# A hybrid encoder layer on one core: recurrence pairs issued in five parts between half lumps of a weight fold, decays in five slices

## The chip, the core and the metric

The kernel runs on one core of a Trainium2 chip. Times are device microseconds from start to end of one execution. The kernel before took 2605.68 us (median of 3 runs, 2604.11 to 2606.04). The core has a matrix engine (PE, whose weight loads PEld overlap its matmuls), a vector engine (DVE), an activation engine (ACT), GpSimd (POOL), and SyncE (SP), whose queue issues nearly all of this kernel's DMAs. Each engine works through its own instructions in order and waits on semaphores for the others.

## What is computed

One encoder layer on 2048 frames of width 1024, in float32: token mixing (sliding-window attention with sinks beside a gated linear recurrence, HGRN2), cross-attention into 256 memory tokens, and a SwiGLU feed-forward part, each with an RMS norm before and after. The change touches the recurrence and the weights of the cross-attention. In short:

```python
def hgrn2(q, f_logit, i, g, lb, onorm_g):          # per head, chunks of 64 frames
    f = lb + (1 - lb) * sigmoid(f_logit); k = 1 - f
    b = cumsum(log(f))                             # within a chunk
    b_mid, b_last = b[31], b[63]
    A = tril((q * exp(b - b_mid)) @ (k * exp(b_mid - b)).T)
    kv = (k * exp(b_last - b)).T @ i
    S = exp(b_last) * S_prev + kv                  # from chunk to chunk
    o = A @ i + (q * exp(b)) @ S_prev
    return rms_norm(o, onorm_g) * silu(g)

def cross_attention(u, m, wq, wk, wv, wo):         # 4 heads of width 256
    p = softmax((u @ wq) @ (m @ wk).T / 16)
    return (p @ (m @ wv)) @ wo
```

## The kernel before

All float32 matmuls of weights are made from three products of a rounded-down and a rest part (`mm3`, L156 to L163: hi x hi, hi x lo, lo x hi), so each weight tile that is loaded (`raw`) is first split: the rounded part `whi` on ACT or POOL (L143, L145), the rest `wlo` on DVE (L146).

The stages follow each other: the input projection of the first half of the frames (`in_first`); the second half's projection (`in_proj`, `in_cols`) beside the first half's attention (`swa`) and recurrence (`hgrn`); the second half's attention; then, in the stage that the change mostly concerns, the second half's recurrence beside the *fold* (`fold_cross`); and then, as a stream of large blocks (`phases`), the output projection, the cross-attention and the feed-forward part.

**The fold** multiplies the memory tokens into the cross-attention's weights ahead of time, since they are fixed: with `kT = wk.T m.T` the scores are `u @ (wq kT)`, and likewise for values. It is a generator that yields after each *lump*: 8 lumps for `kT` (tiles `mT`, 24 matmuls of 256 columns each, L161 to L163, into a bank of kind s or h), 8 lumps for `wq kT` (24 matmuls on the tiles `kv`, two banks, stored to `qk_d`), 8 for the values, and 8 for the values with `wo` (L330 to L332, stored to `vo_d`).

**The recurrence** goes over pairs of chunks (128 frames, numbers n = 8 to 15 in the second half). One step of its generator issues the state of the last pair (`hgrn_state`: L808 on PE, L809 on POOL, L810 on DVE), the front of the next pair (`hgrn_front`), the last part of the pair before (`hgrn_last`: L838 transposes, L839, the store of `sg` to `y_d`), and the output of the last pair (`hgrn_out`: L820 and L821 on PE, four squares with sums on ACT at L825, L827 and L829 on POOL for the root, and L830 on DVE, which reads the output's bank and writes `on`). The front loads `k1`, `qq`, `kk`, `v` from `z_d`, scales on POOL (L774 `qq`, L786 `q6`, L789 `kk`), makes the scores on PE (L781) with a masked copy (L782 DVE, L783 ACT), and transposes `kk` (L792) and `v` (L797), whose copies `kt` and `vt` ACT makes (L794, L799).

Banks of PSUM come in four kinds, g, t, s and h, of two each; the second half's recurrence takes g and t in turn, the fold s and h. In a pair, the kind g serves L808, one half of L781, L792 and L838; the kind t serves the other half of L781, L797, and the output. Single tiles in SBUF serve `k1`, `kk`, `v`, `sg`, `on` and `kt`; `qq`, `q6` and `vt` have two, the raw weights and their parts three.

Before the change the loop of this stage runs one recurrence step and then two lumps of the fold:

```python
for _ in self.hgrn(range(NPB, NT), "gt"):     # L247
    for _ in range(2):
        next(fold)
```

What the Python code issues is not yet the engines' order: the tile layer (`TileContext` with its own timeline, L1648) records all instructions and decides the order on each engine when the program is built. It also places the semaphores.

**The decays** (`decays`, L626 to L649) make, for one head and one half of the frames, the logarithm, its running sum within chunks, and the exponentials `G`, `G1`, `e1` and `e2`. In the first half they are issued from the `after` generator of a projection block (L563), which the stream of blocks advances step by step.

Of the kernel before, what the change touches and what calls it, by code (L numbers as in the profile page):

```python
# [14 lines left out]
AF = mybir.ActivationFunctionType  # L15
# [33 lines left out]
class Layer:  # L49
# [103 lines left out]
        self.split(raw, hi, lo, engine)  # L153
        return (hi.rearrange("p (k c) -> p k c", k=KT), lo.rearrange("p (k c) -> p k c", k=KT))

    def mm3(self, ps, pairs):  # L156

        nc = self.nc
        n = len(pairs)
        for i, ((ah, al), (bh, bl)) in enumerate(pairs):  # L160
            nc.tensor.matmul(ps, ah, bh, start=(i == 0), stop=False)  # L161
            nc.tensor.matmul(ps, ah, bl, start=False, stop=False)  # L162
            nc.tensor.matmul(ps, al, bh, start=False, stop=(i == n - 1))  # L163
# [33 lines left out]
    def mix(self):  # L197
        tc, I = self.tc, self.I
        kw = dict(reuse_waits="tile")
        with contextlib.ExitStack() as left:  # L200
# [18 lines left out]
            with tc.tile_pool(name="sw", bufs=1, side="right", **kw) as self.sw:  # L219
                self.zero_tiles()  # L220
                swa = self.swa(range(NPB), "st")
                hgrn = self.hgrn(range(NPB), "h")
                cols = self.in_proj(1, u)
                for _ in range(2):
                    next(cols)
                for _ in swa:
                    next(hgrn)
                    next(cols)
                for _ in hgrn:
                    pass  # L230
                jobs = self.jobs()
                sums = self.w_sums()
                swa = self.swa(range(NPB, NT), "sth")
                for i, _ in enumerate(swa):
                    next(cols)
                    if i:
                        self.mark()
                        for _ in range(4):
                            next(sums, None)
                for _ in cols:  # L240
                    pass
                for _ in sums:
                    pass
            phases = self.phases(jobs, None, lambda: self.io_tile("z"))
            with tc.tile_pool(name="xp", bufs=1, side="right", **kw) as self.xp:
                fold = self.fold_cross()
                for _ in self.hgrn(range(NPB, NT), "gt"):  # L247
                    for _ in range(2):
                        next(fold)
                for _ in range(8):  # L250
                    next(phases)
                for _ in fold:
                    pass
# [20 lines left out]
    def fold_cross(self):  # L274
# [9 lines left out]
        def projected(w):  # L284
            dst = [ph.tile([P, KT, M], F32R, tag=f"kv{i}", name=f"kv{i}_{self._n}") for i in range(2)]
            for j in range(KT):
                wh, wl = self.wcols(w, j, "A")
                ps = self.bank("sh"[j % 2])[:, :M]
                self.mm3(ps, [((wh[:, k, :], wl[:, k, :]), (mT[0][:, k, :], mT[1][:, k, :])) for k in range(KT)])
                nc.scalar.activation(dst[0][:, j, :], ps, AF.Copy)  # L290
                nc.vector.tensor_tensor(dst[1][:, j, :], ps, f32(dst[0][:, j, :]), ALU.subtract)
                yield dst
# [9 lines left out]
        for d in range(KT):  # L302
            th, tl = self.wcols(self.I["wq_x"], d, "A")
            o = self.io_tile("x")
            for q in range(2):
                ps = self.bank("sh"[q])
                for r in range(2):
                    h = 2 * q + r
                    self.mm3(ps[:, r * M:(r + 1) * M],
                             [((th[:, j, :], tl[:, j, :]), (kT[0][:, j, :], kT[1][:, j, :])) for j in (2 * h, 2 * h + 1)])  # L310
                sl = slice(q * 512, (q + 1) * 512)
                nc.scalar.activation(o[:, sl], ps, AF.Copy, scale=gx[:, d:d + 1])
            self.store(self.qk_d[d * P:(d + 1) * P, :], o)
            yield
        for vT in projected(self.I["wv_x"]):
            yield
        for h in range(4):
# [204 lines left out]
    def in_block(self, ca, cb, beside, get, between):  # L522
# [40 lines left out]
        def after():  # L563
# [2 lines left out]
            c0 = ca * P  # L566
            if C_FH <= c0 < C_IH:
                e = self.pair_tile()
                self.decays(0, (c0 - C_FH) // P, z[0][:, 0, :], e[:, 0, :], e[:, 1, :])
                yield  # L570
                yield
                for j in range(2):
                    sl = slice(j * 512, (j + 1) * 512)
                    nc.vector.scalar_tensor_tensor(z[0][:, 1, sl], z[0][:, 1, sl], -0.5 * float(P) ** -0.5,
                                                   e[:, 0, sl], ALU.mult, ALU.mult)
            for i, c in enumerate((ca, cb)):
                self.store(self.z_d[c * P:(c + 1) * P, 0:TB], z[0][:, i, :])
            for _ in range(3 if C_FH <= c0 < C_IH else 4):
                yield
            for n, p in x:  # L580
                self.store_transposed(self.un_d, n, self.transposed(p[:, 0, :], p[:, 1, :]))
# [11 lines left out]
    def in_cols(self, b, u, cols, e1):  # L593
# [24 lines left out]
        for i, c in enumerate(cols):  # L618
            c0 = c * P
            if C_FH <= c0 < C_IH:  # L620
                e1 = self.io_tile("x")
                self.decays(b, (c0 - C_FH) // P, z[i], e1, self.io_tile("u"))
            self.store(self.z_d[c0:c0 + P, b * TB:(b + 1) * TB], z[i])
        return e1

    def decays(self, b, h, f, e1, e2):  # L626

        nc = self.nc
        NCB = TB // 64
        nc.scalar.activation(e1, f, AF.Ln)  # L630
        for s in range(TB // 512):
            sl = slice(s * 512, (s + 1) * 512)
            nc.vector.tensor_tensor_scan(e2[:, sl], self.reset.rearrange("p a b -> p (a b)"), e1[:, sl], 0.0,
                                         ALU.mult, ALU.add)
# [5 lines left out]
                                ALU.mult, ALU.mult)  # L640
        gs = self.small("d_g", NCB)
        nc.gpsimd.tensor_tensor(gs, mid, self.dl[:, h, b * NCB:(b + 1) * NCB], ALU.add)
        g2 = gs.rearrange("p (n c) -> p n c", c=2)
        nc.scalar.activation(self.G1[:, b * NPB:(b + 1) * NPB, h], g2[:, :, 1], AF.Exp)
        nc.gpsimd.tensor_tensor(g2[:, :, 1], g2[:, :, 0], g2[:, :, 1], ALU.add)
        nc.scalar.activation(self.G[:, b * NPB:(b + 1) * NPB, h, :], g2, AF.Exp)
        nc.scalar.activation(e1, e2, AF.Exp)
        nc.scalar.activation(e2, e2, AF.Exp, scale=-1.0)
        nc.vector.scalar_tensor_tensor(f, f, 1.0, e2, ALU.subtract, ALU.mult)  # L649

    def swa_front(self, n, kinds):
# [96 lines left out]
            nc.vector.tensor_tensor(ys[a], pr[a], ys[a], ALU.add)  # L748
        self.store(self.y_d[n, :, 0:4], ys)

    def hgrn_front(self, n, kinds):
        nc, ph = self.nc, self.hg
        t0 = n * P
        z = self.z_d
# [22 lines left out]
        for i in range(2):  # L777
# [4 lines left out]
            nc.vector.copy_predicated(at[:, hs, :], self.cmask.unsqueeze(1).broadcast_to([P, 2, P]), ps[:, :, 0:P])  # L782
            nc.scalar.activation(at[0:64, hs, 64:P], ps[0:64, :, P:192], AF.Copy)  # L783

        q6 = new("q6", 2)
        nc.gpsimd.tensor_tensor(q6.rearrange("p h (c t) -> p h c t", t=64), q1.rearrange("p h (c t) -> p h c t", t=64),  # L786
                                self.G[:, n, :, :].unsqueeze(3).broadcast_to([P, 4, 2, 64]), ALU.mult)
# [9 lines left out]
            nc.tensor.transpose(ps[:, h * P:(h + 1) * P], v[:, h, :], self.ident)  # L797
        vt = new("vt", 2)
        nc.scalar.activation(vt, ps.rearrange("p (h t) -> p h t", h=4), AF.Copy)  # L799
        return q6, at, kt, vt  # L800

    def hgrn_state(self, n, kinds, kt, vt):
        nc, ph = self.nc, self.hg
# [39 lines left out]
    def hgrn(self, pairs, kinds):  # L843

        f, o = {}, {}
        for n in itertools.chain(pairs, (None, None)):
# [2 lines left out]
                W = self.hgrn_state(m, kinds, kt, vt)  # L849
            else:  # L850
                m = None
            if n is not None:
                f[n] = self.hgrn_front(n, kinds)
            if o:
                l, v = o.popitem()
                self.hgrn_last(l, kinds, *v)
            if m is not None:
                o[m] = self.hgrn_out(m, kinds, q6, at, vt, W)
            yield
# [792 lines left out]
```

## Time and profile before

| | us |
|---|---|
| median of 3 runs | 2605.68 |
| the profiled execution | 2605.43 |
| its span, first to last instruction | 2603.6 |
| PE busy | 2526.8 |
| DVE busy | 1744.2 |
| ACT busy | 1262.3 |
| POOL busy | 473.4 |
| second half's recurrence beside the fold (PE's first L781 to its last L332) | 645.7 to 794.6 |

In the views below, times are us from the start of the span. A timeline's row has start, duration, engine, line, operation, output and inputs, and in brackets the time that the engine was idle before it and what released it. A row of the chain of waits has start, duration and the link. PE's matmuls are pipelined: a row's duration is longer than its distance to the next (256 columns: 0.28 us long, 0.12 apart). PEclk is the share of its full clock that PE was granted.

### The profile page before, as it was taken

What the parts mean: (1) busy time and instruction counts of PE and PEld (TensorE: products, weight loads), DVE (VectorE), ACT (ScalarE), POOL (GpSimd) and SP (SyncE); (2) the same over time, 40 slices, a digit from 0 to 9 for tenths busy, and PEclk for the clock granted to TensorE, in tenths of its full rate; (3) what the DMA queues carried; (4) which work ended last, traced back from release to release, by engine and by line L of the source; (5) the groups of instructions that cost most, each with busy time, mean ns of one, the idle gap of its engine ahead of it and who ended that gap; (6) DMA issues with size and microseconds to landing.
All of it is one profiled execution on the core that took longest, in us unless ns stands there. A gap on an engine that the chain in (4) does not pass through costs nothing.

```text
span 2603.6 us, 34511 instructions
## 1 busy us (share of the span) xinstructions
PE 2526.8 (97%) x12160; PEld 2112.8 (81%) x12160; DVE 1744.2 (67%) x2773; ACT 1262.3 (48%) x2641; POOL 473.4 (18%) x651
## 2 busy tenths in 40 slices
PE   7989999999998999999989999999999999999998
PEld 6878788878897777888878888888888888888786
DVE  7675578887555568786885655576666656664756
ACT  5463366655554556565573333354333335443443
POOL 4240343320321324223320000000000000000022
PEclk9999999999999999999999999999999999999999
DMA  5434655484876998756994532353556434576798
GB/s 186 142 121 166 208 157 173 131 265 158 265 253 219 281 318 265 228 193 173 306 282 145 164 128 73 105 187 114 168 181 230 148 107 168 175 225 176 229 226 210
DMA packets 286350, 497.88 MB, mean 191 GB/s; under 512 B 20576, under 2 KB 143456, under 8 KB 286176
## 3 DMA queue, kind: packets, MB, share of 16 engines
q1 hardware_dynamic: 275520, 456.87, 52.4%
q0 software_dynamic: 10656, 38.80, 8.0%
q8 instruction: 96, 1.57, 0.2%
q14 instruction: 78, 0.64, 0.1%
HBM read 328.87 MB, written 166.72 MB: 190 GB/s over the span
## 4 chain that ended last, share of the span: by engine, by line
PE 80%; DMA 8%; DVE 4%; issue 3%; POOL 2%; ACT 2%; SPq 0%; DVEq 0%; POOLq 0%; ACTq 0%
PE psm L1018 22%; PE psm L1020 22%; PE psm L1019 22%; PE psg L161 2%; PE psg L163 2%; PE psg L162 2%; DMA row<-in_x_dram 1%; PE pss L1270 1%; DMA row<-h_d 1%; ACT junk L1355 1%; DMA x<-in_w_out_dram 1%; DVE S L885 1%; DMA h_d<-row 1%; DMA pair<-in_x_dram 1%; DMA kk<-z_d 1%
## 5 line engine op out<-in xcount | busy, mean ns | idle before, releaser
L1018 PE MATMUL psm<-T,S 128*128 128x512 f32 x2664 | 1034.9, 392 | 24.6 <-ACT S L882 13.5
L1019 PE MATMUL psm<-T,S 128*128 128x512 f32 x2664 | 1041.1, 391 | 0.0
L1020 PE MATMUL psm<-T,S 128*128 128x512 f32 x2664 | 1036.1, 391 | 3.8 <-DVE S L885 3.8
L1018 PEld LDWEIGHTS psm<-T,S 128*128 128x128 f32 x2664 | 502.2, 189 | 132.7 <-ACT S L882 15.3
L1020 PEld LDWEIGHTS psm<-T,S 128*128 128x128 f32 x2664 | 501.9, 188 | 111.0 <-DVE S L885 6.9
L1019 PEld LDWEIGHTS psm<-T,S 128*128 128x128 f32 x2664 | 502.3, 189 | 103.0
L882 ACT ACTIVATE S<-sum 128x512 fp32r<-128x512 f32 (+1 forms) x338 | 208.1, 619 | 341.4 <-PE psm L1020 333.1
L885 DVE TENSOR_TENSOR S<-sraw,S 128x512 fp32r<-128x512 f32 (+1 forms) x311 | 214.2, 696 | 223.4 <-ACT S L882 213.4
L885 DVE TENSOR_TENSOR S<-sum,S 128x512 fp32r<-128x512 f32 (+1 forms) x404 | 276.8, 689 | 81.6 <-ACT S L882 63.7
L1033 ACT ACTIVATE part<-psm 128x512 f32<-128x512 f32 x297 | 175.1, 592 | 178.0 <-PE psm L1020 172.8
L882 ACT ACTIVATE S<-sraw 128x512 fp32r<-128x512 f32 (+1 forms) x272 | 166.8, 617 | 156.0 <-PE psm L1020 143.0
L1384 POOL DMA_DIRECT2D row<-y_d x28 | 25.0, 892 | 1132.5 <-DMA sraw<-hid_d 964.5
L1355 ACT ACTIVATE junk<-row 128x512 f32<-128x512 f32 x160 | 99.7, 625 | 118.2 <-DVE row L1377 34.9
L885 DVE TENSOR_TENSOR T<-row,T 128x1024 fp32r<-128x1024 f32 x104 | 123.1, 1191 | 30.5 <-ACT T L882 30.2
L161 PE MATMUL psg<-u,whi 128*128 128x512 f32 x352 | 141.1, 401 | 1.6 <-POOL whi L145 1.6
L163 PE MATMUL psg<-u,wlo 128*128 128x512 f32 x352 | 139.5, 396 | 0.9 <-DVE wlo L146 0.9
L162 PE MATMUL psg<-u,whi 128*128 128x512 f32 x352 | 139.6, 396 | 0.0
L882 ACT ACTIVATE T<-row 128x1024 fp32r<-128x1024 f32 x104 | 105.7, 1027 | 20.7 <-DMA row<-in_w_down_dram 10.3
L884 POOL TENSOR_SCALAR S<-sum 128x512 fp32r<-128x512 f32 x66 | 50.5, 765 | 238.7 <-PE psm L1020 148.3
L1536 DVE TENSOR_TENSOR part<-psm,part 128x512 f32<-128x512 f32 x66 | 45.4, 688 | 65.3 <-PE psm L1020 65.2
L146 DVE TENSOR_TENSOR wlo<-raw,whi 128x1024 fp32r<-128x1024 f32 x54 | 68.7, 1271 | 29.1 <-ACT whi L143 22.4
L1527 DVE TENSOR_TENSOR row<-psm,part 128x512 f32<-128x512 f32 x66 | 45.4, 689 | 57.6 <-PE psm L1020 57.5
(329 smaller groups left out, 3651.3 us busy)
## 6 DMA issues: line engine op xcount, KB each, us to landing
sraw<-in_w_gate_dram SPq DMA_DIRECT2D x44, 512.0 KB, 4.9
sraw<-in_w_up_dram SPq DMA_DIRECT2D x44, 512.0 KB, 4.8
hid_d<-row SPq DMA_DIRECT2D x44, 512.0 KB, 2.7
h_d<-row SPq DMA_DIRECT2D x32, 512.0 KB, 6.9
y_d<-row SPq DMA_DIRECT2D x32, 512.0 KB, 3.8
sraw<-hid_d SPq DMA_DIRECT2D x32, 512.0 KB, 5.2
row<-h_d POOLq DMA_DIRECT2D x30, 512.0 KB, 7.5
row<-y_d POOLq DMA_DIRECT2D x28, 512.0 KB, 7.3
```

Of the source, the lines that this page charges most:

```text
L146: nc.vector.tensor_tensor(lo, raw, f32(hi), ALU.subtract)
L161: nc.tensor.matmul(ps, ah, bh, start=(i == 0), stop=False)
L162: nc.tensor.matmul(ps, ah, bl, start=False, stop=False)
L163: nc.tensor.matmul(ps, al, bh, start=False, stop=(i == n - 1))
L882: self.nc.scalar.activation(hi, raw, AF.Copy)
L884: self.nc.gpsimd.tensor_scalar(hi, raw, 1.0, 1.0, ALU.mult, ALU.mult)
L885: self.nc.vector.tensor_tensor(lo, raw, f32(hi), ALU.subtract)
L1018: nc.tensor.matmul(ps, s[:, 0, k, :], t[:, 0, k, :], start=st, stop=False, **kw)
L1019: nc.tensor.matmul(ps, s[:, 0, k, :], t[:, 1, k, :], start=False, stop=False, **kw)
L1020: nc.tensor.matmul(ps, s[:, 1, k, :], t[:, 0, k, :], start=False, stop=sp, **kw)
L1033: nc.scalar.activation(t, ps, AF.Copy)
L1355: self.nc.scalar.activation(junk, a, AF.Square, scale=float(D) ** -0.5, accum_out=to)
```

## The change

Four things are edited.

1. `hgrn` yields five times for a pair: after the state, in the middle of the front (which is now a generator itself and leaves its results in `f`), after the front, after the last part, and after the output. The first half's loop takes five of them where it took one.
2. The fold yields half lumps: `mm3` gets a `part` and issues half of its matmuls, `projected` yields between the halves, and the lumps of `wq kT` yield after each bank.
3. The loop of the second half advances the fold by one half lump after each of the four later parts of a pair, and by none after the state. So a pair still has four half lumps.
4. `decays` is a generator of five slices (four yields). In the first half the block's `after` advances it step by step; it had two bare yields behind the whole, and three before its next part, and now has one there. Within `decays`, the exponential `e1` comes ahead of `G`, and `G` after `e2`. `in_cols` runs it at once.

```diff
-    def mm3(self, ps, pairs):
+    def mm3(self, ps, pairs, part=None):
...
         for i, ((ah, al), (bh, bl)) in enumerate(pairs):
+            if part is not None and i * 2 // n != part:
+                continue
             nc.tensor.matmul(ps, ah, bh, start=(i == 0), stop=False)
...
                 for _ in swa:
-                    next(hgrn)
+                    for _ in range(5):
+                        next(hgrn)
                     next(cols)
...
-                for _ in self.hgrn(range(NPB, NT), "gt"):
-                    for _ in range(2):
+                for i, _ in enumerate(self.hgrn(range(NPB, NT), "gt")):
+                    for _ in range(1 if i % 5 else 0):
                         next(fold)
...
-                self.mm3(ps, [((wh[:, k, :], wl[:, k, :]), (mT[0][:, k, :], mT[1][:, k, :])) for k in range(KT)])
+                for part in range(2):
+                    if part:
+                        yield dst
+                    self.mm3(ps, [((wh[:, k, :], wl[:, k, :]), (mT[0][:, k, :], mT[1][:, k, :])) for k in range(KT)],
+                             part)
...
-            self.store(self.qk_d[d * P:(d + 1) * P, :], o)
-            yield
+                if q:
+                    self.store(self.qk_d[d * P:(d + 1) * P, :], o)
+                yield
...
-                self.decays(0, (c0 - C_FH) // P, z[0][:, 0, :], e[:, 0, :], e[:, 1, :])
-                yield
-                yield
+                yield from self.decays(0, (c0 - C_FH) // P, z[0][:, 0, :], e[:, 0, :], e[:, 1, :])
...
-            for _ in range(3 if C_FH <= c0 < C_IH else 4):
+            for _ in range(1 if C_FH <= c0 < C_IH else 4):
                 yield
...
         nc.scalar.activation(e1, f, AF.Ln)
+        yield
...
         nc.gpsimd.tensor_tensor(gs, mid, self.dl[:, h, b * NCB:(b + 1) * NCB], ALU.add)
+        yield
         g2 = gs.rearrange("p (n c) -> p n c", c=2)
         nc.scalar.activation(self.G1[:, b * NPB:(b + 1) * NPB, h], g2[:, :, 1], AF.Exp)
         nc.gpsimd.tensor_tensor(g2[:, :, 1], g2[:, :, 0], g2[:, :, 1], ALU.add)
+        nc.scalar.activation(e1, e2, AF.Exp)
+        yield
+        nc.scalar.activation(e2, e2, AF.Exp, scale=-1.0)
         nc.scalar.activation(self.G[:, b * NPB:(b + 1) * NPB, h, :], g2, AF.Exp)
-        nc.scalar.activation(e1, e2, AF.Exp)
-        nc.scalar.activation(e2, e2, AF.Exp, scale=-1.0)
+        yield
         nc.vector.scalar_tensor_tensor(f, f, 1.0, e2, ALU.subtract, ALU.mult)
...
-    def hgrn_front(self, n, kinds):
+    def hgrn_front(self, n, kinds, f):
...
             nc.scalar.activation(at[0:64, hs, 64:P], ps[0:64, :, P:192], AF.Copy)
 
+        yield
         q6 = new("q6", 2)
...
-        return q6, at, kt, vt
+        f[n] = q6, at, kt, vt
+        yield
...
                 W = self.hgrn_state(m, kinds, kt, vt)
             else:
                 m = None
-            if n is not None:
-                f[n] = self.hgrn_front(n, kinds)
+            yield
+            yield from self.hgrn_front(n, kinds, f) if n is not None else (None, None)
             if o:
                 l, v = o.popitem()
                 self.hgrn_last(l, kinds, *v)
+            yield
             if m is not None:
                 o[m] = self.hgrn_out(m, kinds, q6, at, vt, W)
             yield
```

More of the change, by code (lines that the diff above doesn't have):

```diff
@@ L621, in in_cols @@
                 e1 = self.io_tile("x")
-                self.decays(b, (c0 - C_FH) // P, z[i], e1, self.io_tile("u"))
+                for _ in self.decays(b, (c0 - C_FH) // P, z[i], e1, self.io_tile("u")):
+                    pass
             self.store(self.z_d[c0:c0 + P, b * TB:(b + 1) * TB], z[i])
```

## The prediction

> **What bounds the kernel now.** I read the page first, then PE's stretches and idle time between 640 and 810 us, then the chain of waits there, then the DMA queue's timeline. The page's chain says who sets the end:
>
> ```profile
> PE 80%; DMA 8%; DVE 4%; issue 3%; POOL 2%; ACT 2%; SPq 0%; DVEq 0%; POOLq 0%; ACTq 0%
> ```
>
> PE sets it, so an edit is worth what it takes from, or adds to, PE's holes. The tile layer chooses each engine's order when the program is built. Set side by side, the built orders of the two kernels are equal, instruction by instruction, in their tiles and in what they wait for, until the second half of the recurrence is under way beside the fold (PE's time 677 us); and they are equal again from the last part of the fold on. Only what lies between can gain or lose. PE's stretches there (us of the stretch, then busy us and instructions of each engine):
>
> ```profile
> core 0: us, PE busy (x) PEld busy (x) DVE busy (x) ACT busy (x) POOL busy (x), PEclk, DMA share, GB/s
> 687.00:692.00 5.00, 4.22 (x33) 3.75 (x33) 4.22 (x7) 0.92 (x3) 2.13 (x2) 1.00 0.46 129
> 701.00:704.00 3.00, 2.65 (x22) 2.30 (x22) 2.74 (x5) 0.69 (x1) 1.60 (x2) 1.00 1.00 325
> 713.00:715.40 2.40, 0.45 (x5) 0.25 (x4) 0.82 (x2) 0.00 (x0) 1.38 (x3) 1.00 0.36 147
> 715.40:719.30 3.90, 3.80 (x19) 3.60 (x20) 2.29 (x4) 1.91 (x6) 1.96 (x2) 0.56 0.89 268
> 720.00:757.00 37.00, 37.00 (x316) 37.00 (x315) 17.35 (x24) 21.99 (x61) 11.93 (x14) 1.00 0.79 259
> 757.00:794.50 37.50, 37.50 (x227) 33.19 (x226) 17.37 (x20) 20.20 (x31) 0.00 (x0) 1.00 0.69 239
> ```
>
> From 720 on PE has no hole. Before that there are three, and a stretch at a granted clock of 0.56 right behind the third. PE stands before the same instruction, the transposition of v (L797):
>
> ```profile
> 702.05 0.63 PE L797 MATMUL pst<-ident,v 128*128 128x128 f32 x4 [0.35 <-issue]
> ...
> 713.10 0.28 PE L163 MATMUL psh<-kv,wlo 128*128 128x256 f32 x1
> 715.33 0.55 PE L797 MATMUL pst<-ident,v 128*128 128x128 f32 x3 [1.95 <-DVE on L830]
> ```
>
> L797 needs a bank of the kind t; there are two, and the one whose turn it is still holds the outputs of the pair before, until DVE's L830 has read them. The chain of waits says why L830 is late, and, by its L808 rows, how long a pair takes:
>
> ```profile
> 697.74 0.89 PE psg L808 x8
> ...
> 704.64 6.79 DMA kk<-z_d
> 711.57 0.61 POOL kk L789
> 712.18 1.00 POOL q L786
> 713.26 0.20 POOL h_vv L827
> 713.54 1.02 POOL h_rs L829
> 714.58 0.70 DVE on L830
> 715.33 0.55 PE pst L797 x3
> ...
> 724.36 0.89 PE psg L808 x8
> ...
> 735.32 0.89 PE psg L808 x8
> ```
>
> L830 waits for L829, and L829 stands on POOL behind L789, which waits for the load of kk. L789 to L830 take 714.58 + 0.70 - 711.43 = 3.85 us from the landing.
>
> **The change part by part.** *The decays in slices, and the five parts in the first half of the recurrence.* No instruction of either stands elsewhere in the built order. Cost 0 from both sides; there is nothing that needs cover.
>
> *The five parts with half lumps, second half.* It adds no instruction and no DMA. For a pair, PE's order was: state (L808), scores (L781), 15 or 16 fold matmuls, v (L797), kk (L792), some 17 fold matmuls, L838, output (L820, L821), 16 fold matmuls. It becomes: L808, L781, 16 fold matmuls, kk, 11 fold matmuls, v, 5, L838, 4, output, 12. So L797 comes 11 fold matmuls and four transpositions later: 11 x 0.117 + 0.44 = 1.7 us (37 us for 316 matmuls; eight of L808's kind take 0.89). In the first pair L838 comes 24 fold matmuls, 2.8 us, later, and with it DVE's L839, SP's store of y_d and what stands on SP behind that store's landing (the loads of sg, k and q). PE wants those a pair later, so the slack is most of 11 us, and I cost it at 0; without that slack it would be up to 2.8. On DVE, L830 moves behind the state's sum (L810) and one split of fold weights (L146); what is now queued behind its wait is one or two short copies, no longer L810 and L146. On POOL, kk goes ahead of q in two pairs. On SP nothing is added; kk's load goes ahead of v's in most pairs, and in the first pair one load of fold weights goes ahead of kk's.
>
> What the holes cost: the pairs from 697.74 to 724.36 took 26.62 us, two undisturbed ones take 2 x (735.32 - 724.36) = 21.92, so 4.70. This has in it the hole of 1.95 and the slow stretch behind it. The pair before lies in the first row of the stretches: 33 matmuls at 316/37 = 8.54 per us need 3.9 of 5 us, so 1.1. Together 5.8 us, and this is all that can be had here, as PE's work stays the same.
>
> Is L797 then late enough? In the pair of the long hole L797 wanted PE at 713.2 and had it at 715.33, 2.1 later; 1.7 of that is covered by its new place. The rest is covered on SP: kk's load at 704.64 stood behind a load of weights that waited for a split on DVE, which stood behind L830. With L830 behind the split, kk's load waits for little more than its buffer, which L792 frees. From the end of L792 to L797 of the next pair PE now has a pair's 11.0 and 11 fold matmuls, 12.3 us, and the loop needs 6.79 + 3.85 = 10.6 and the issue. L792 itself, now in front, waits for L789: 6.79 + 0.14 + 0.61 = 7.5 of some 10.5 us. So the second and third hole close whole: -4.7.
>
> In the first pair the load of weights is in front, and its wait is known:
>
> ```profile
> 678.34 1.22 DVE L146 TENSOR_TENSOR wlo<-raw,whi 128x1024 fp32r<-128x1024 f32 x1
> ```
> ```profile
> 677.33 0.38 SPq L75 DMA_DIRECT2D kk<-z_d  x1
> 677.80 0.82 SPq L75 DMA_DIRECT2D v<-z_d  x1
> 679.58 0.34 SPq L75 DMA_DIRECT2D raw<-in_wq_x_dram  x1
> ```
>
> The load of weights goes at 679.6, as before; kk's, at 677.33 so far, goes behind it at 680.0, 2.7 us later. From there I take kk's landing time; the trace has no such load behind that one, so these rows (median us to landing last) bound it:
>
> ```profile
> sraw<-y_d SPq DMA_DIRECT2D x6, 512.0 KB, 8.4
> ...
> kk<-z_d SPq DMA_DIRECT2D x7, 256.0 KB, 6.4
> ```
>
> At 6.4 L830 ends at 680.0 + 6.4 + 3.85 = 690.3. What PE has done before L797 starts from the end of L781:
>
> ```profile
> 686.98 0.81 PE L781 MATMUL pst<-qq,k 128*128 128x192 f32 x4
> ```
>
> That is 687.8 at the latest (until there the moved instructions are the same in number), then 27 fold matmuls and four transpositions: L797 at 691.4. No hole. At 8.4 L830 ends at 692.3 and the hole is 0.9, nearly all of this pair's 1.1. I take 0.2, nearer to the row of the same load.
>
> The interleaving makes 11 more changes from recurrence to fold matmuls on PE (33 for 22). One costs what this shows:
>
> ```profile
> 690.64 0.63 PE L792 MATMUL psg<-ident,kk 128*128 128x128 f32 x4
> 691.02 0.37 PE L161 MATMUL pss<-mT,whi 128*128 128x256 f32 x1
> 691.23 0.28 PE L162 MATMUL pss<-mT,whi 128*128 128x256 f32 x1
> ```
>
> The first matmul holds PE for 0.21 instead of 0.12, but the four transpositions before it took 0.38 instead of 0.44 (half of L808's 0.89): between 0 and 0.09, I take 0.02, so +0.2 (0 to 1.0).
>
> Does a shorter fold reach the end? Its last products lead to the first load of the next phase:
>
> ```profile
> 794.75 0.32 SPq L78
> ...
> 795.17 5.98 DMA sraw<-y_d
> 801.17 0.64 ACT S L882
> ```
>
> That load stands on SP behind a store of the fold's last result, so it moves with the fold, and all of it is passed on. The slow clock behind this gap can differ by about 1 us either way, as the slow stretch need not begin at the same place of the gap.
>
> Sum: -5.8 + 0.2 + 0.2 = -5.4. The profiled execution took 2605.43 us, so 2600.0. The median of the runs shown is 2605.68, 0.25 above it; 0.2%, about what a measurement of this kernel can tell from no change, is 5.2 us, so the border lies at 2600.5, inside the forecast's own spread of 2599.0 to 2601.7.
>
> The slow stretch is 1.7 of the sum: 3.9 us at a clock of 0.56. [...]
>
> **The rivals.** (1) *The holes move.* The load of weights ahead of kk costs 8.4 in the first pair, and one more pair keeps a hole of about 1 us, since the DMA share is 1.00 at 701 to 704 and the same bytes now go in less time. For it: those rows. Against: the pairs from 720 run at 259 GB/s without a hole. -5.8 + 0.9 + 1.0 + 0.2 = -3.7: 2601.7.
>
> (2) *The slow stretch isn't the hole's.* If something else slows the clock there, 1.7 us stay: 2600.0 + 1.7 = 2601.7. Against: it begins within 0.6 us of the hole's end. [...]
>
> (3) *It does nothing.* The built order says that most of the edit doesn't reach the chip, and the rest could be taken back in the gap before the next phase if its load came from a busy queue: 8.4 instead of 5.98 gives back 2.4, and with (1) it leaves -1.3: 2604.1.
>
> (4) *Slower: kk in front.* L792 now stands before v, and all fold matmuls of the pair stand behind it in PE's queue. Should kk land later than 12.3 - 3.85 = 8.4 us after L792, every pair has a hole again, and each hole near 2 us brings a slow stretch. At 10.2 us five pairs have 1.8 + 1.7 each: +17.5 - 5.4, so 2617; over 0.2% slower from about 9.5 us. For it: 325 GB/s at 701, and no row of the trace says how the queue does under more. Against: the slowest kk on the chain took 6.79.
>
> **How the numbers follow.** Forecast 0.62, (1) 0.12, (2) 0.05, (3) 0.09, (4) 0.12. Two thirds of the forecast lie under 2600.5: faster 0.42. The rest of it and (1) to (3): same 0.46. (4): slower 0.12. The range, to hold the time 8 times in 10, is 2598.6 (all 5.8, and 1 us less of slow clock behind the gap) to 2605.6, which leaves out (4) and little else.
>
> **What would show it.** Right: PE without a hole at L797 between 687 and 720, no slow stretch there, pairs of 11.0 us between L808 rows throughout, the fold's last L332 at about 789, and the gap behind it as long as it was. Wrong: a hole before L792 (kk late), a hole before L797 in the first pair (the load of weights), a slow stretch in the fold without a hole, or any difference before 677 us.

## The result, and the profile after

| | before | changed |
|---|---|---|
| median of 20 runs each, in one series | 2608.55 us (2603.32 to 2611.53) | 2604.9 us (2599.26 to 2611.11) |
| ratio, 95% interval | | 0.9985 (0.9979 to 0.9991) |
| the profiled execution | 2605.43 | 2603.6 |
| its span | 2603.6 | 2601.7 |

The changed kernel is 0.15% faster, some 3.9 us, with an interval of 2.3 to 5.5 us; by the bound of 0.2% that is no difference, but it is clear of zero. The forecast was 2600.0 (2598.6 to 2605.6); the median lies 0.7 us under the top of that range. The lines of the changed kernel are a dozen further down: the transposition of v, L797, is now L809; the state L808 is L821; kk's transposition L792 is L804; `on` (L830) is L843; L838 is L851; the fold's last product L332 is L340.

First the windows that the prediction showed of before, in the profile of after (microseconds of the stretch, its length, busy time and count of PE, PEld, DVE, ACT, POOL, then PE's granted clock, the DMA share and GB/s):

```profile
core 0: us, PE busy (x) PEld busy (x) DVE busy (x) ACT busy (x) POOL busy (x), PEclk, DMA share, GB/s
687.00:692.00 5.00, 5.00 (x44) 5.00 (x43) 2.92 (x6) 2.31 (x6) 2.01 (x2) 1.00 0.80 247
701.00:704.00 3.00, 3.00 (x28) 3.00 (x27) 1.58 (x5) 2.08 (x5) 0.48 (x1) 1.00 1.00 286
713.00:715.40 2.40, 2.40 (x23) 2.40 (x22) 0.93 (x1) 2.40 (x6) 0.00 (x0) 1.00 0.99 298
715.40:719.30 3.90, 3.90 (x36) 3.90 (x35) 1.02 (x3) 2.95 (x12) 0.61 (x1) 1.00 0.92 273
720.00:757.00 37.00, 35.65 (x302) 35.30 (x301) 17.86 (x24) 19.95 (x51) 11.95 (x14) 1.00 0.76 257
757.00:790.40 33.40, 33.40 (x191) 28.83 (x189) 14.59 (x16) 18.45 (x30) 0.00 (x0) 1.00 0.68 240
```

The three old holes are gone and so is the slow stretch: 36 matmuls at a clock of 1.00 between 715.40 and 719.30, where before had 19 at 0.56. But the stretch from 720 on, which had no hole, now has 35.65 busy us of 37.00 and 302 matmuls instead of 316. The chain of waits of after says where:

```profile
696.31 0.89 PE psg L821 x8
...
707.27 0.89 PE psg L821 x8
...
718.24 0.89 PE psg L821 x8
...
724.05 0.68 issue
724.73 0.63 PE pst L809 x4
...
730.07 0.89 PE psg L821 x8
...
735.88 0.67 issue
736.55 0.63 PE pst L809 x4
...
741.91 0.89 PE psg L821 x8
```

Two pairs of 10.96 us are followed by two of 11.83, each with a hole ahead of L809, the same instruction that had the holes before. The profile calls the wait "issue", but the timeline has DVE's `on` (L843), which frees v's bank, end just before the transposition:

```profile
723.94 0.69 DVE L843 TENSOR_TENSOR on<-pst,h_rs 128x512 f32<-128x512 f32 x1 [2.88 <-POOL h_rs L842]
```

And the chain at the fold's end:

```profile
789.87 0.25 PE pss L340
...
790.37 0.32 SPq L78
...
790.78 6.01 DMA sraw<-y_d
796.82 0.64 ACT S L896
```

The load starts 4.39 us earlier than before's (795.17), and its 6.01 us are the 5.98 of before: the gap was passed on whole.

### The profile page after: what moved, and what is told of

The parts are those of the page before. It is cut to its first block, busy times and chain, and to the rows that moved or that the text cites. A ratio compares the mean times of both kernels' runs of the same rounds, so it can differ in the third digit from the quotient of the medians.

```text
span 2601.7 us, 34516 instructions
## 1 busy us (share of the span) xinstructions
PE 2528.0 (97%) x12160; PEld 2115.2 (81%) x12160; DVE 1746.0 (67%) x2773; ACT 1262.0 (49%) x2641; POOL 466.6 (18%) x651
## 4 chain that ended last, share of the span: by engine, by line
PE 80%; DMA 8%; DVE 4%; issue 3%; POOL 2%; ACT 2%; SPq 0%; DVEq 0%; POOLq 0%; ACTq 0%
PE psm L1032 22%; PE psm L1034 22%; PE psm L1033 22%; PE psg L163 2%; PE psg L164 2%; PE psg L165 2%; DMA row<-in_x_dram 1%; PE pss L1284 1%; DMA row<-h_d 1%; DMA u_d<-row 1%; DMA h_d<-row 1%; DMA x<-in_w_out_dram 1%; ACT junk L1369 1%; DMA pair<-in_x_dram 1%; DMA extra<-qk_d 0%
```

## The experiments

The table has, from each run's profile, the time from the first to the sixth state matmul beside the fold (the start of eight matmuls of L821's kind, 685.16 and 741.75 in the changed kernel), from the first state to the last product of the fold (790.18), and from there to the end of the span. The ratio is to the kernel before in the same series, from 6 runs (e5), 7 (e1) or 11 to 12 of the others; runs that share a number in the last column were taken on the same chip.

| run | first to sixth state | first state to fold's end | fold's end to span's end | ratio, 95% interval | series |
|---|---|---|---|---|---|
| before | 60.69 | 109.13 | 1809.0 | | 0 |
| changed | 56.59 | 105.02 | 1811.6 | 0.9985 (0.9979 to 0.9991) | 0 |
| e1 parts alone | 57.45 | 105.89 | 1808.6 | 0.9977 (0.9966 to 0.9987) | 1 |
| e2 v later, two lumps | 61.25 | 109.69 | 1810.4 | 0.9998 (0.9988 to 1.0007) | 1 |
| e3 second buffer for sg | 58.18 | 106.61 | 1811.4 | 0.9980 (0.9972 to 0.9989) | 1 |
| e4 second buffer for kk | 55.73 | 104.16 | 1811.6 | 0.9995 (0.9986 to 1.0004) | 1 |
| e5 separate tile for the store | 54.83 | 103.26 | 1808.2 | 0.9972 (0.9961 to 0.9983) | 2 |
| e6 the same in the kernel before | 57.31 | 105.75 | 1810.9 | 0.9983 (0.9973 to 0.9993) | 2 |
| e7 v earlier, two lumps | 60.35 | 108.78 | 1813.1 | 0.9995 (0.9987 to 1.0004) | 2 |
| e8 decays alone | 62.89 | 111.33 | 1810.8 | 0.9993 (0.9983 to 1.0004) | 2 |
| e9 parts alone again | 56.26 | 104.70 | 1806.5 | 0.9982 (0.9974 to 0.9991) | 3 |
| e10 separate tile again | 54.83 | 103.26 | 1813.3 | 0.9981 (0.9972 to 0.9990) | 3 |
| e11 changed, second h_rs | 57.26 | 105.70 | 1812.0 | one run | 3 |
| e12 separate tile, second h_rs | 54.86 | 103.31 | 1813.3 | one run | 3 |

**e1 and e9: the parts without the slices.** The edit takes the slices of the decays out of the changed kernel and leaves the rest:

```diff
-                yield from self.decays(0, (c0 - C_FH) // P, z[0][:, 0, :], e[:, 0, :], e[:, 1, :])
+                self.decays(0, (c0 - C_FH) // P, z[0][:, 0, :], e[:, 0, :], e[:, 1, :])
+                yield
+                yield
...
```

> The five parts and the half lumps alone, the decays in one piece as before. Theory (everything comes from the second half of the recurrence beside the fold): this is the changed kernel on every engine, so the ratio to the kernel before is the changed kernel's, 0.9985 within 0.0008, and in the profile the three old holes before the transposition of v are gone and two of 0.8 us stand at 724 and 736 us. Last L808-line matmul of state some 4.4 us earlier than before. Rival (the slices of the decays give part of it): ratio nearer 1.000, at least 1 us of the 3.9 us missing. Second question: between the fold's end and the program's end the profile of the changed kernel gave back half of its 4.4 us. If this give-back belongs to the program, it is here again within 0.3 us; if it hangs on where the slow stretches of PE's clock fall in one execution, it is another number here, by 1 us or more.

> The changed kernel again (parts alone), beside the separate tile on one chip. Pairs of 11.83 us from the second or third on, first to sixth state 56.5 to 57.6 us; ratio to the kernel before 0.9977 to 0.9985.

Ratio 0.9977, and 0.9982 in e9: the parts alone give the changed kernel's gain. The fold's stage has no hole in its first pairs, as in the changed kernel, but here three pairs of 11.83 us (the third to the fifth), where two were expected, and in e9 one of 11.52 and one of 11.83 (56.26 us for the five, a little under the expected 56.5). In e1's profile the whole stage lies later, so the last state comes 1.6 us before that of the kernel before, not the expected 4.4. The three profiles are of the same instructions in the same order on every engine, so this differs between executions. So does what comes behind the fold: 1811.6, 1808.6 and 1806.5 us. Of its lead of 4.4 us the changed kernel's profile gave back 2.6 there; e1's gained 0.4 us on before's. What is given back is the execution's, not the change's.

**e8: the slices alone.**

> The slices of the decays alone. Theory: every engine's instructions are those of the kernel before, so ratio 1.0000 within 0.0010, and in the profile a hole before v in the third pair of 1.5 to 2.5 us again. How far the times at the same instruction lie apart between this profile and that of the kernel before says what one execution differs from another. Rival (the slices do something): a difference of over 2 us that the other runs of the kernel before do not show.

The ratio 0.9993 has 1 in its interval: no effect that these runs can tell. The profile of this second execution of before's instructions has the holes again, but not of the same length, nor in the same pairs:

```profile
690.73 0.66 PE L800 MATMUL pst<-ident,v 128*128 128x128 f32 x4 [1.49 <-DVE on L833]
...
704.72 0.63 PE L800 MATMUL pst<-ident,v 128*128 128x128 f32 x4 [0.80 <-ACT x L312]
...
741.12 1.05 PE L800 MATMUL pst<-ident,v 128*128 128x128 f32 x4 [2.37 <-DVE on L833]
```

(L800 is before's L797, L833 its L830.) The long one is in the fifth pair, not the third. The expectation of 1.5 to 2.5 us in the third pair was too narrow; the stage as a whole is 2.2 us longer than in the first profile. Up to the fold's end the change is worth about 5 us: the mean of before's two profiles is 110.2, that of the changed kernel's three 105.2.

**e7 and e2: where v stands.** The fold's lumps come whole and twice a pair; `range(t[i % 5])` half lumps follow the part i, with t = (0, 0, 2, 0, 2) in e7 and (0, 2, 0, 0, 2) in e2:

```diff
-                    for _ in range(1 if i % 5 else 0):
+                    for _ in range((0, 0, 2, 0, 2)[i % 5]):
                         next(fold)
```

> The fold's matmuls in two whole lumps, one behind the transpositions and one behind the output: v is transposed 9 to 12 fold matmuls behind the scores (kernel before 15 or 16, changed kernel 27). Theory (v's place decides): the holes before v are there as in the kernel before, 2 to 3 us together or more, first to sixth state 59 to 62 us (before 60.7), ratio 0.9995 to 1.001. Rival (finer parts are what helps, wherever v stands): holes under 1 us together, ratio 0.9985.

As the theory had it (the ratio, 0.9995, too): with v 9 to 12 fold matmuls behind the scores the holes are there in spite of the finer parts, and the stage is as long as before's (60.35):

```profile
702.48 0.65 PE L809 MATMUL pst<-ident,v 128*128 128x128 f32 x4 [1.52 <-DVE on L843]
...
726.57 0.66 PE L809 MATMUL pst<-ident,v 128*128 128x128 f32 x4 [1.75 <-DVE on L843]
```

> The fold's matmuls come in two whole lumps, one between the scores and the transpositions, one after the output, instead of four halves. From the output to the transposition of v PE then has 48 fold matmuls (changed kernel 39, before 31). Theory (a hole before v is there where v's place is too near to the output of the pair before, whose bank it takes): no hole before v in any pair, the two of 0.83 us in the changed kernel too closed, by 9 x 0.117 = 1.05 us more distance; fold's end 5 to 6 us before the kernel before, ratio 0.9975 to 0.9985. Rival (it takes the half lumps at four places): holes come back somewhere, ratio 0.999 or above.

Here the theory failed, and what the rival had said came about (holes come back, 0.9998). With v later than in the changed kernel the pairs take 11.34, 11.39, 11.71, 13.86 and 12.96 us, and the stage is the longest but one in the table. The timeline of e2 around the longest pair:

```profile
720.24 0.43 SPq L78 DMA_DIRECT2D y_d<-sg  x1
...
724.20 0.61 POOL L801 TENSOR_TENSOR kk<-kk,G 128x256 f32<-128x256 f32 x1 [2.41 <-DMA kk<-z_d]
...
727.21 0.69 DVE L843 TENSOR_TENSOR on<-pst,h_rs 128x512 f32<-128x512 f32 x1 [7.00 <-POOL h_rs L842]
728.60 0.63 PE L804 MATMUL psg<-ident,kk 128*128 128x128 f32 x4 [1.80 <-issue]
728.86 0.37 SPq L75 DMA_DIRECT2D sg<-z_d  x1
```

The hole is now ahead of kk's transposition, which stands behind the same chain (kk on POOL, h_rs, `on`, and DVE's read of the state's bank behind `on`), and SP's load of sg comes 8.6 us behind the store of y_d, whose landing it waits for. A late place for v is no cure if what v waits for comes later with every pair. So what does v wait for? SP's column of the changed kernel (e1, where it has settled) gave the next theory. L798 is POOL's multiply of kk, L840 is `on`, L806 the transposition of v:

```profile
719.97 0.65 SPq L78 DMA_DIRECT2D y_d<-sg  x1
...
726.39 0.37 SPq L75 DMA_DIRECT2D sg<-z_d  x1
...
727.40 0.45 SPq L75 DMA_DIRECT2D raw<-in_wv_x_dram  x1
...
727.96 0.37 SPq L75 DMA_DIRECT2D kk<-z_d  x1
...
734.72 1.44 POOL L798 TENSOR_TENSOR kk<-kk,G 128x256 f32<-128x256 f32 x1 [7.01 <-PE psg L789]
...
738.57 0.69 DVE L840 TENSOR_TENSOR on<-pst,h_rs 128x512 f32<-128x512 f32 x1 [2.87 <-POOL h_rs L839]
739.36 0.63 PE L806 MATMUL pst<-ident,v 128*128 128x128 f32 x4 [0.68 <-issue]
```

The next store of this loop is issued at 743.62. From store to store it goes: 6.4 us until the store has landed and sg may be overwritten, 1.6 until kk's load is issued behind those of sg, k and weights, 6.8 until kk is there, 3.9 to `on`, 5.1 through `on`, the transpositions and DVE's product to the next store. Together 23.65 us, twice 11.83; two pairs of PE's work take 21.9. Since every pair has a store, any two pairs would add up so; that these steps are what sets their length is a theory until the wait in it is taken away, as e5 does.

**e3 and e4: more buffers.**

```diff
-        sg = ph.tile([P, 4, P], F32, tag="sg", name=f"sg{n}")
+        sg = ph.tile([P, 4, P], F32, tag="sgb" if n >= NPB and n % 2 else "sg", name=f"sg{n}")
```

> The changed kernel with a second buffer for sg in the second half, so that its load waits no longer for the store of y_d to land, and the loads of kk, k and q that stand behind it on SP are issued up to 1.4 us earlier. Theory (the two new holes of 0.83 us come from kk landing late, POOL's multiply of kk then lying beside the DVE split of fold weights and taking 1.58 us, not 0.61): kk's load issued at about 711.8, not 713.2; both holes closed; 1.7 us less than the changed kernel at the fold's end, ratio to the kernel before 0.9978 (changed kernel 0.9985). Rival (POOL is slowed in any case, or kk lands late for another reason, the crowded DMA queues): the holes stay within 0.3 us, ratio 0.9985.

The rival's numbers, but no test of it: pairs of 10.98, 11.82, 11.85, 11.69 and 11.84 us, four long ones. In the built order each load of sg went up by a pair and stands behind the store that frees the other buffer; it still waits for a landing (16.8 us in four waits between 690 and 740 us), and k, weights and kk wait behind it. The edit did not take the wait away, so it does not decide between the two. (Its ratio of 0.9980 is within what e1 and e9 have.)

```diff
-        kk = get(new("kk"), C_FH)
+        kk = get(new("kkb" if n >= NPB and n % 2 else "kk"), C_FH)
```

> The changed kernel with a second buffer for kk in the second half: its load waits no longer for the transposition of the kk before. Theory: kk is there a pair ahead, POOL's multiply starts with its turn, no hole before v at all: as with the second buffer of sg, 1.7 us less at the fold's end, ratio 0.9978. Rival (DVE's and POOL's own order makes the hole, not the load): two holes of 0.8 us stay, ratio 0.9985.

Beside the fold four of five pairs are 10.97 to 10.99 us and one is 11.84: neither the theory's (no hole) nor the rival's (two). The ratio of 0.9995 seems to come from another place: the extra tile also changed the order ahead of the fold, where the first state beside it starts at 694.81 us, not 685.16, and PE stood there before kk's first transposition:

```profile
660.22 0.65 PE L804 MATMUL psg<-ident,kk 128*128 128x128 f32 x4 [3.84 <-ACT atz L794]
```

**e5, e6 and e10: the store from a tile of its own.** This takes the wait itself away, since sg is free as soon as DVE has read it:

```diff
+        yo = sg if n < NPB else self.hg.tile([P, 4, P], F32, tag="yo", name=f"yo{n}", bufs=1)
-        nc.vector.scalar_tensor_tensor(sg, ps.rearrange("p (h t) -> p h t", h=4), self.onorm[:, 0:1], sg,
+        nc.vector.scalar_tensor_tensor(yo, ps.rearrange("p (h t) -> p h t", h=4), self.onorm[:, 0:1], sg,
                                        ALU.mult, ALU.mult)
-        self.store(self.y_d[n, :, 4:8], sg)
+        self.store(self.y_d[n, :, 4:8], yo)
```

> The changed kernel, but in the second half the result of L852 goes to a tile of its own, and y_d is stored from there; sg is then free when DVE has read it, and its load waits no longer for the store of y_d to land (the second buffer of sg did not do this: the tile layer only moved the load up to the next store). New theory, a loop of two pairs: store of y_d (landing after 5.4 to 7.3 us) -> loads of sg, k, q, weights and kk one behind the other on SP (3.4 us) -> landing of kk (6.1 to 6.9) -> POOL kk, q, h_vv, h_rs (0.6 + 1.0 + 0.2 + 1.0) -> DVE on (0.7) -> transposition, DVE sg, next store (3.9): 22 to 24 us, where two pairs of PE's work take 21.9. It explains the pairs of 11.83 us: 23.66 for two. It expects here: no pair over 11.1 us, no hole over 0.3 us before v, the time from the first to the sixth state at 54.9 us (changed kernel 56.6, the parts alone 57.5, second buffer of sg 58.2), and 1.7 to 3.3 us less at the end: ratio to the kernel before 0.9968 to 0.9977. Rival (kk lands late because the DMA queues are full, whatever SP does): pairs of 11.8 us stay, ratio 0.998.

The order of the instructions is the changed kernel's on PE, DVE, ACT and POOL; only SP's differs. Every pair takes 10.97 us; first to sixth state 54.83 (54.9 expected), ratio 0.9972 (0.9968 to 0.9977 expected). The timeline of e5:

```profile
706.09 0.33 SPq L78 DMA_DIRECT2D y_d<-yo  x1
...
706.96 0.46 SPq L75 DMA_DIRECT2D sg<-z_d  x1
...
711.69 0.69 DVE L843 TENSOR_TENSOR on<-pst,h_rs 128x512 f32<-128x512 f32 x1
...
714.60 0.60 PE L809 MATMUL pst<-ident,v 128*128 128x128 f32 x4
```

The load of sg follows the store by 0.87 us, not 6.4, and `on` ends 2.2 us before v needs its bank. With this wait taken away the long pairs are gone, as the loop has it; the rival's pairs of 11.8 us did not come.

> The changed kernel with the separate tile again. Theory (loop of two pairs over SP cut): pairs of 10.97 us, first to sixth state 54.8 us, fold's end 1.7 to 2.6 us before the changed kernel's in the same call when the shift up to the first state is taken off; ratio to the kernel before 0.0007 to 0.0010 under the changed kernel's. Rival (what the fold gains is always given back behind it): the same ratio as the changed kernel within 0.0003.

In the stage the same again, to 0.01 us: 54.83, and 1.44 us less up to the fold's end than e9's 104.70 (1.7 to 2.6 expected; e9 had only one hole and a half). At the end of the program nothing of it can be seen: 0.9981 against 0.9982, each uncertain by 0.0009, which is 2.3 us; that is the ratio that the rival gave. In e10's profile the part behind the fold is 6.8 us longer than in e9's, but also 5.1 longer than in e5's, which is the same program. Whether the separate tile shortens the whole by 1.4 us is therefore not shown; that it closes the holes is.

> The same separate tile in the kernel before, its recurrence in whole pairs. Theory of the prediction (its hole of 1.95 us comes from v standing too early, and from kk behind a load of weights that waits for a DVE split): the store's landing is not what is waited for, a hole before v in the third pair stays at over 1 us, ratio 0.999 to 1.000. Rival (the loop over SP binds the kernel before too, and v's place is of no account): no holes, first to sixth state in 55.5 us or less, ratio 0.9975 to 0.998, as much as the change itself.

Both were half right. A hole before v stayed in the second pair, but the stage lost 3.4 us against before's first profile and 5.6 against e8, and the ratio is 0.9983, about that of the change itself. The row of the hole in e6 and DVE's row that ends it (the profile names ACT, but `on` ends at 703.16):

```profile
702.47 0.69 DVE L830 TENSOR_TENSOR on<-pst,h_rs 128x512 f32<-128x512 f32 x1 [3.75 <-POOL h_rs L829]
703.26 0.63 PE L797 MATMUL pst<-ident,v 128*128 128x128 f32 x4 [1.22 <-ACT x L312]
```

So the wait for the store's landing had cost the kernel before something as well. SP's column of before has it ahead of the long hole's kk:

```profile
694.36 0.33 SPq L78 DMA_DIRECT2D y_d<-sg  x1
...
699.81 0.36 SPq L75 DMA_DIRECT2D sg<-z_d  x1
...
703.71 0.34 SPq L75 DMA_DIRECT2D raw<-in_wq_x_dram  x1
...
704.64 0.45 SPq L75 DMA_DIRECT2D kk<-z_d  x1
```

SP stood 5.0 us for the store's landing ahead of the load of sg and 2.2 for DVE ahead of that of the weights; the prediction named only the second. v's place and SP's waits are two levers on the same hole.

**e11 and e12: one microsecond more on POOL.** The power that makes h_rs is done twice in the second half:

```diff
-        nc.gpsimd.tensor_tensor(rs, vv, self.mhalf[:, 0:4], ALU.pow)
+        for _ in range(1 if n < NPB else 2):
+            nc.gpsimd.tensor_tensor(rs, vv, self.mhalf[:, 0:4], ALU.pow)
```

> The changed kernel with the power that makes h_rs done twice in the second half (the second time over the first, same numbers): 1.0 us more on POOL between the landing of kk and on. The tile layer sets v 3 to 6 fold matmuls later and the transposition of on directly behind it. Theory (loop of two pairs): 23.66 + 1.01 - 5 x 0.117 = 24.1 us for two pairs, 12.0 for one; first to sixth state 58 to 60 us. Rival (a wait inside one pair): 11.83 + 1.01 - 3 x 0.117 = 12.5 us a pair.

> The same second power in the kernel with the separate tile. There on is ready 2.2 us before v needs its bank (711.69 + 0.69 against the next transposition at 703.64 + 10.97 in the run of the separate tile). Theory (loop cut, so a delay on POOL is only a delay): pairs of 10.97 us as without it, first to sixth state 54.9 us. Rival (POOL's chain itself binds): pairs longer by 0.5 us or more.

With the loop cut (e12) the extra microsecond costs nothing: pairs of 10.96 to 10.98, 54.86 us. In the changed kernel (e11) it was expected to make the loop longer and did not: pairs of 11.31, 10.96, 11.27, 12.56 and 11.17, the last two together 23.73 where 24.1 was forecast (and one of them 12.56, where the rival had 12.5 for all), 57.26 us in all, within what the changed kernel's own profiles show (56.26 to 57.45). The tile layer had moved v 3 to 6 fold matmuls later and the transposition of `on` up to it; whether that hid the extra time was not tried. So e12 agrees with the loop, and the size that the loop theory gave for e11 was wrong; both are single runs.

## Why the prediction was right, and where it was not

*The slices of the decays, 0.* Right as far as measured: 0.9993 with 1 in the interval.

*The three holes close, -5.8.* Right. From state to state the first three pairs took 12.14, 11.67 and 14.94 us before and 10.99, 10.97 and 10.97 after: 38.75 - 32.93 = 5.8. The mechanism named, v's place, is borne out by e7, which has the holes again with v further to the front. It is not the only one: e6 shortens before's stage by 3.4 us with v where it was, and e2, with v later still, has holes ahead of kk. How much of the 5.8 is v's place alone the runs do not separate.

*The first pair, +0.2.* 0: the pair takes 10.99 us. kk's load went at 679.34, not 680.0, and `on` ended at 688.7, ahead of v at 690.98.

*The extra switches on PE, +0.2.* An undisturbed pair takes 10.97 us where it took 10.96, so at most 0.05 for five.

*The store of y_d, 0.* This is the term that was wrong. The prediction had seen that L838 and with it the store of y_d go later, and the loads behind that store's landing with them, and said: "PE wants those a pair later, so the slack is most of 11 us, and I cost it at 0". PE does want k and q a pair later. But kk's load stands in the same queue behind them, and from kk the way goes over POOL and DVE to v's bank and back to the store: a loop of two pairs, with no slack of a pair in it. With this term fell the sentence that kk's load "waits for little more than its buffer, which L792 frees": in the fourth pair of after the transposition that frees it starts at 722.16, the load only at 725.28, behind that of sg. The loop took 23.65 us in e1 against PE's 21.9. In the profile of after it cost 2 x (11.83 - 10.97) = 1.7 us, in the other two profiles of the same instructions 2.6 and 1.4. e5 and e10 show it by taking the wait away: not one long pair. So the sign "pairs of 11.0 us between L808 rows throughout" came true for the first three pairs only.

*All is passed on.* Right at the gap: the last product of the fold is 4.38 us earlier than before (790.18 against 794.56), the load behind it 4.39. Behind the gap PE runs at half clock from 801.85 to 808.03 before and from 797.50 to 801.12 after: half of 6.2 - 3.6 us, by estimate 1.3 us gained (in after's profile 9 matmuls fall into 797.70 to 801.12 at 0.50, 16 into the next 3.41 us at 1.00), where about 1 us either way was allowed. The slow stretch did not begin at the same place of the gap: at 797.79 before, 2.8 us behind the end of the fold's last product, at 794.29 after, 3.7 behind.

*The sum.* -5.4 was forecast. At the fold's end -4.4 was measured in that pair of profiles, of which 0.3 was there before the stage's first state; the terms as measured give -5.8 + 1.7 = -4.1. Between the means of three and two profiles the stage is 5.0 shorter, and over 20 runs of each the whole is 3.9 shorter (2.3 to 5.5). The forecast of 2600.0 us lies 4.9 below the median for a second reason: it was made against one execution of 2605.43, and the 20 runs of before have their median 3.1 us above that. That 2604.9 lies in the range says little, for the range reached up to 2605.6, over the time of that one execution: no change at all would have lain in it too. What can be judged is the difference and the terms.

*The rivals.* (2), the slow stretch isn't the hole's: refuted where it stood, as the hole went and the slow stretch with it; in e8 the long hole came in the fifth pair, and the slow stretch stands there, from 741.24. (4), kk in front: no hole at kk in the changed kernel; e2 has one there, of 1.80 us, with the clock at 1.00 in the 3.41 us from 728.50, so not each hole near 2 us brought a slow stretch. (1), the holes move: its -3.7 is nearest to the 20 runs, and holes did move, but not by its mechanism: not in the first pair, and not for a full DMA share, since e5 has no hole with the same bytes. (3), it does nothing: out by the ratio, whose interval ends at 0.9991 (-1.3 us would be 0.9995), though its 2604.1 us is nearest to the median, which is luck, as it too was counted from 2605.43.

## What to carry to other kernels

When an instruction is moved, ask of each load in the queue behind it which engine's chain it starts, not only when the matrix engine wants its data; the slack is that of the shortest loop that closes through the queue. A store from the tile that the next load fills puts the store's landing into that loop; a tile of its own took it out (the load of sg went 6.4 us after the store in e1, 0.87 in e5), where a second buffer only moved the waiting load (in e3 16.8 us in four waits). For effects of a few microseconds compare the stage's own length in several profiles, since the rest of the program differs by more than that from one execution to the next (1806.5 to 1811.6 us in three profiles of the same instructions).

## What the runs showed of the hardware

*The stretches at half clock stood on a grid of 3.41 us.* In the profiles of before and of the changed kernel the stretches at half clock between 100 and 2590 us, seven and nine, are 3.41 us long or two or three times that, and within one profile they all start on one grid of that step, to 0.01 us. Two stretches of 3.41 us each around a hole, of before, e7 and e2:

```profile
712.46:715.87 3.41, 1.46 (x11) 1.02 (x9) 1.29 (x3) 0.00 (x0) 1.92 (x3) 1.00 0.44 175
715.87:719.28 3.41, 3.31 (x17) 3.34 (x17) 1.82 (x3) 1.89 (x6) 1.95 (x1) 0.50 0.99 297
```
```profile
724.26:727.67 3.41, 1.66 (x14) 1.27 (x13) 1.85 (x3) 0.00 (x0) 1.84 (x4) 1.00 0.75 272
727.67:731.08 3.41, 3.41 (x18) 3.41 (x17) 1.26 (x3) 2.38 (x6) 1.48 (x1) 0.50 0.84 258
```
```profile
725.09:728.50 3.41, 1.71 (x15) 1.51 (x13) 1.29 (x3) 0.00 (x0) 1.92 (x3) 1.00 0.89 354
728.50:731.91 3.41, 2.63 (x22) 2.42 (x23) 1.81 (x3) 1.83 (x4) 1.95 (x1) 1.00 0.64 174
```

PE busy for 1.46 or 1.66 of 3.41 us is followed by 3.41 us at 0.50, 1.71 is not, though e2's hole of 1.80 us is as long as e7's of 1.75. Two other holes differ in where they lie on the grid: before's of 2.09 us up to 887.21 goes over a step of its grid (886.53), and the clock is 1.00 before and after that step; the changed kernel's of 2.02 us up to 999.00 lies between two steps, and from 999.09 to 1002.50 the clock is 0.50. Counted over these two kernels' profiles from 660 to 2590 us (idle time of PE as the distance from one matmul's start to the next, less 0.112, 0.118, 0.163 or 0.234 us for one of 128, 256, 192 or 512 columns), 30 steps of the grid at full clock have 0.9 us idle or more. The ten with 2.17 us or more are each followed by one at half clock, none of the twenty with 1.98 or less is.

That is also one reason why the part behind the fold differs between executions of the same instructions. In the changed kernel's profile:

```profile
927.42:930.83 3.41, 0.73 (x7) 0.76 (x8) 0.00 (x0) 0.77 (x3) 0.00 (x0) 1.00 1.05 270
930.83:934.24 3.41, 3.41 (x12) 2.73 (x10) 2.29 (x4) 2.51 (x7) 0.00 (x0) 0.50 0.74 287
```

This hole is 2.94 us long; in e9, the same instructions, PE is busy for 3.28 us of the first of these stretches and for all of the second, both at 1.00. In the changed kernel's profile a slow stretch follows the hole of 2.02 us up to 999.00 too; in e9 PE is busy for 2.31 us from 995.68 to 999.09 and for 1.88 from there to 1002.50, both at 1.00. Between the fold and 1400 us the changed kernel's profile has 27.3 us at half clock, before's 20.5. Half of the difference, an estimate of what it costs, is 3.4 us; behind the fold the one is 2.6 us longer (1811.6 against 1809.0), so the clock is not all that differs there.

*POOL's multiply of kk took longer beside a DVE split.* The multiply takes 0.61 us by itself (at 707.47 in the changed kernel), but where a DVE split had begun before it or with it, it takes longer. In the changed kernel:

```profile
719.85 1.21 DVE L146 TENSOR_TENSOR wlo<-raw,whi 128x1024 fp32r<-128x1024 f32 x1
719.95 1.58 POOL L801 TENSOR_TENSOR kk<-kk,G 128x256 f32<-128x256 f32 x1 [2.56 <-DMA kk<-z_d]
```

1.11 us of overlap and 1.58 us. In the next pair, at 731.77, 1.12 goes with 1.59; in e1 1.22 with 1.70 (at 722.64) and 0.98 with 1.44 (734.72); in e8 0.78 with 1.25 (686.32): 0.46 to 0.48 more than the overlap. Where 0.13 us of a split was left (the changed kernel's at 684.85), the multiply kept its 0.61. Why the two go together, no run shows. The two long pairs of after have this delay, and so have the fourth and fifth of e1: up to 1.1 us of the loop above. It is not what makes a pair long by itself: e2's longest pair took 13.86 us with a multiply of 0.61 (724.20).
